# One encoder trunk: probabilities times V in plain FP32 for the mLSTM and dilated heads

## The chip, the cores and the metric

The kernel runs on one core of a Trainium2 chip. The metric is the device time of one execution in microseconds (us), taken as the median of several executions. The profiled execution is a run of its own and has its own time.

## The reference

Two layers of a hybrid encoder trunk act on two groups of tokens with the same weights, 256 of a prompt and 512 of a sample, 1024 channels each. Everything is FP32. Cut to what matters here, a layer is

```
z = rmsnorm(x) @ w_in                       # q, k, v of three head groups, gates
ya = dilated attention, 4 heads of 64       # mixture of three windows, softmax
yb = mLSTM, 4 heads of 64                   # gated weights, forward plus backward, no softmax
yc = grouped attention, 8 query heads on 2 k/v heads
x += concat(ya, yb, yc) @ w_out
x += cross attention into 256 memory tokens, 4 heads
x += (silu(conv3(gate)) * val) @ w_down     # gate, val = rmsnorm(x) @ w_up
```

In each head a matrix P of (queries x keys) is formed and multiplied with V (keys x 64). P is a softmax in the dilated, grouped and cross heads, and a gated, normalised score matrix in the mLSTM.

## The kernel before

Channels lie on the partitions and the 768 tokens along the columns: first the 256 of the prompt, then the 512 of the sample. `STREAMS` holds both as (start, length), the sample first. A projection is done in the type FP32R, in which one matmul carries only a part of the bits of an FP32 number. Each operand is therefore split into a high part (a cast on ScalarE, `hi_op`) and the rest (a subtraction on VectorE, `tt`), and three matmuls are summed: high times high, high times rest, rest times high (`mm_chunks`, L208).

`attend` (L367) does one head on one stream. It forms the scores block by block in the PSUM bank S (two buffers), lets `soft` turn them into P in SBUF (tiles of 512 columns from the FP32 arena), and for the mLSTM waits until all rows are there and scales them (`settle_p`). Then, for each key block, it transposes P on TensorE into the bank T (two buffers, L392), casts the 512 columns into `ph` on ScalarE (L395) and subtracts on VectorE into `pl` (L396). Two FP32R matmuls accumulate into the bank Y (one buffer): V times `ph` (L400) and V times `pl` (L401). The weights are 128 wide: `v_tokens` (L340) has put V's high part into 64 of the columns and its rest into the other 64, in the order that depends on the head's place e in its pair. So one half of Y's partitions holds the product with the high part and the other that with the rest, and the end of `attend` adds them: a copy on ScalarE (L405) and an addition on VectorE (L406). For 512 tokens there are four blocks T and four key blocks; for 256 tokens one block T holds both key blocks.

A layer runs its heads in this order: grouped (c0, c1), mLSTM (b0, b1), dilated (a0, a1), two heads to a pair for b and a. `ahead` (L353) writes a later pair's projections first in the program but gives the attention of the pair before a higher priority, so that projections fill the time between the steps of an attention. The order on each engine is fixed ahead of the run by a scheduler that simulates the kernel. Buffers come from arenas, lists of free column ranges in one large tile, of which the range freed longest ago is taken: `af` in FP32 (18 x 768 columns), `ar` in FP32R for the operands of matmuls, and `asm` of 4 x 512 columns for `ph` and `pl` alone. The feed-forward stage cuts its own arenas out of the same two large tiles (`ffn`, L1011), and one of them, `fw`, runs to the end of the FP32 tile.

V is projected by `v_proj` (L619): 10 and 11 are the column blocks of the mLSTM's V, 4 and 5 those of the dilated heads, 17 that of the grouped heads.

Of the kernel before, what the change touches and what calls it, by code (L numbers as in the profile page):

```python
# [9 lines left out]
F32 = mybir.dt.float32  # L10
# [25 lines left out]
N_IN = 21  # L36
N_HID = 21
HT = T // 2
HOT = 2000
CHUNKS = ((0, 1),) + tuple((c, c + 2) for c in range(1, 21, 2))  # L40

# [3 lines left out]
R_COLS = 18 * 768  # L45
S_COLS = 4 * 512
PREP = 7 * 512
F_COLS = 18 * 768
N_PAR = 143

K_ID, K_TRI, K_IND = 0, 128, 384
# [57 lines left out]
def trunk_kernel(ctx, tc, xT, memT, w_in, w_out, w_xq, w_xkv, w_xo, w_up, w_dn, w_dnt, par, fin_g, cst, fmk, tabs,  # L109
# [227 lines left out]
                      sub="%s%d%d" % (name, n, k % 4))  # L337
        return xh_s, xl_s

    def v_tokens(zv, nt, vv, site):  # L340
        for c0, n in (STREAMS if nt == 6 else ((0, 512),)):
            ps = small_ps(site, "vps")
            m = n // 128
            j0 = c0 // 128
            for i in range(m):
                PE.transpose(ps[:, i * 128:(i + 1) * 128], zv[:, c0 + i * 128:c0 + (i + 1) * 128], ident)
            for e in range(2):
                src = ps[:, :n].rearrange("p (i h d) -> p i h d", h=2, d=64)[:, :, e]
                a, b = 64 * e, 64 - 64 * e
                A.copy(vv[e][:, j0:j0 + m, a:a + 64], src)  # L350
                tt(vv[e][:, j0:j0 + m, b:b + 64], src, vv[e].bitcast(F32)[:, j0:j0 + m, a:a + 64], ALU.subtract)
# [15 lines left out]
    def attend(qs, q0, nq, KH, KL, k0, nk, vv, vt0, e, y, y0, soft, settle_p=None):  # L367
# [14 lines left out]
            held.append(pt)  # L382
        if settle_p:
            settle_p(ptiles)
        yps = bank("Y", "yps")
        nkt = nk // 128
        nb = 512 // n
        for kb in range(0, nkt, nb):
            t = bank("T", "t")
            for j in range(nb):  # L390
                for i in range(nq):
                    PE.transpose(t[:, j * n + i * 128:j * n + (i + 1) * 128],  # L392
                                 ptiles[i][:, (kb + j) * 128:(kb + j + 1) * 128], ident)
            ph, pl = asm.tile(512), asm.tile(512)
            hi_op(pick("ph_" + SITE[0], "A"), ph, t)  # L395
            tt(pl, t, ph.bitcast(F32), ALU.subtract)  # L396
            for j in range(nb):
                kt = kb + j
                w = vv[:, vt0 + kt]
                PE.matmul(yps[:, :n], w, ph[:, j * n:(j + 1) * n], start=kt == 0, stop=False)  # L400
                PE.matmul(yps[:, :n], w, pl[:, j * n:(j + 1) * n], start=False, stop=kt == nkt - 1)  # L401
            asm.free(ph, pl)
        af.free(*held)
        yo = y[64 * e:64 * e + 64, y0:y0 + n]
        hi_op(pick("yo_" + SITE[0], "A"), yo, yps[64 - 64 * e:128 - 64 * e, :n])  # L405
        tt(yo, yps[64 * e:64 * e + 64, :n], yo, ALU.add)  # L406

# [110 lines left out]
    def mixers(l, xt, x_dram, stats):  # L518
# [100 lines left out]
        def v_proj(t):  # L619
            zv = ft()  # L620
            proj(w_in[l, t], xh, xl, ev_to(zv, "v%d" % t), sub="w_v%d" % t)
            vv = [rtl(), rtl()]
            v_tokens(zv, 6, [tok(v) for v in vv], "v%d" % t)
            af.free(zv)
            return vv
# [43 lines left out]
        def c_attn(g, qr):  # L669
# [4 lines left out]
            for hh in range(4):  # L674
# [2 lines left out]
                           plain_soft(den[:, hh, c0 // 128:(c0 + n) // 128, g],  # L677
                                      lambda i, ni, hh=hh, c0=c0: rq8[:, c0 // 128 + i:c0 // 128 + i + ni, hh]))
                ar.free(qs[hh])
            ar.free(K, vv)  # L680

        def stacks(qq, kk):
            out = []
# [50 lines left out]
        def b_attn(pb, sv):  # L734
            SITE[0] = "b%d" % pb
            sts, vv, rows = sv
            for e in range(2):
                qs, K = sts[e]
                hd = 2 * pb + e
                for c0, n in STREAMS:  # L740
                    gb = rows[e][:, 2 * c0:2 * c0 + 2 * n].rearrange("p (d k) -> p d k", d=2)
                    attend(qs, c0, n // 128, K[:, :T], K[:, T:], c0, n, tok(vv[e]), c0 // 128, e, yt[5 + pb], c0,
                           *b_soft(gb, c0, n, hd))
                af.free(rows[e])
                ar.free(qs, K, vv[e])

        def b_soft(gb, c0, n, hd):
            nq, t0 = n // 128, c0 // 128
# [74 lines left out]
        def a_attn(pg, sv, order, last=True):  # L823
# [5 lines left out]
                       mask_soft(C["fm"], den[:, 4 + pg, c0 // 128:(c0 + n) // 128, e]))  # L829
            if last:  # L830
                for e in range(2):
                    ar.free(*sts[e], vv[e])

        ths = []

# [608 lines left out]
```

## Time and profile before

| | us |
|---|---|
| median of three executions | 2137.96 (2136.34 to 2138.89) |
| profiled execution, whole | 2145.01 |
| its span, first to last instruction | 2143.2 |
| TensorE (PE) busy | 2003.8 |
| VectorE (DVE) busy | 1841.7 |
| ScalarE (ACT) busy | 1061.7 |

PE busy counts a matmul from its start to its modelled end, and the next one starts before that. So 100% is reached while matmuls still follow each other at their own pace, and the distance between two starts is the better measure of what a matmul costs. The granted clock is the share of 2.4 GHz that TensorE was given, as a mean over a stretch: 1.00 is 2.4 GHz throughout, 0.50 is 1.2 GHz throughout.

### The profile page before, as it was taken

What the parts mean: (1) busy time and instruction counts of PE and PEld (TensorE: products, weight loads), DVE (VectorE), ACT (ScalarE), POOL (GpSimd) and SP (SyncE); (2) the same over time, 40 slices, a digit from 0 to 9 for tenths busy, and PEclk for the clock granted to TensorE, in tenths of its full rate; (3) what the DMA queues carried; (4) which work ended last, traced back from release to release, by engine and by line L of the source; (5) the groups of instructions that cost most, each with busy time, mean ns of one, the idle gap of its engine ahead of it and who ended that gap; (6) DMA issues with size and microseconds to landing.
All of it is one profiled execution on the core that took longest, in us unless ns stands there. A gap on an engine that the chain in (4) does not pass through costs nothing.

```text
span 2143.2 us, 31059 instructions
## 1 busy us (share of the span) xinstructions
PE 2003.8 (93%) x11280; PEld 1782.8 (83%) x11280; DVE 1841.7 (86%) x3822; ACT 1061.7 (50%) x2119; POOL 7.8 (0%) x32
## 2 busy tenths in 40 slices
PE   7989989998899999999999897999988999999997
PEld 5878768787789999999888775777877999999995
DVE  8787887867999999999977868778779999999998
ACT  4257767547533333333534667565665333333342
POOL 0000000000000000000000000000000000000000
PEclk8989989999999999999999998999999999999998
DMA  5433335342132212212254314343421222222202
GB/s 179 138 82 101 96 89 124 110 132 80 50 90 79 67 62 72 74 63 88 65 179 117 92 44 107 99 111 123 124 64 56 83 70 69 70 69 70 69 30 79
DMA packets 62953, 190.94 MB, mean 89 GB/s; under 512 B 8072, under 2 KB 11400, under 8 KB 62032
## 3 DMA queue, kind: packets, MB, share of 16 engines
q1 hardware_dynamic: 62800, 188.96, 30.1%
q8 instruction: 89, 1.46, 0.3%
q14 instruction: 64, 0.52, 0.1%
HBM read 145.97 MB, written 10.71 MB: 73 GB/s over the span
## 4 chain that ended last, share of the span: by engine, by line
PE 74%; DVE 16%; ACT 4%; DMA 3%; issue 2%; SPq 1%; POOL 0%; DVEq 0%; ACTq 0%
PE rps L1105 8%; PE rps L1107 8%; PE rps L1106 8%; PE rps L1148 5%; PE rps L1149 5%; PE rps L1150 5%; PE prS L213 4%; PE prS L214 4%; PE prS L215 4%; DVE arena_f L158 4%; PE t L392 3%; PE prP L213 2%; PE prP L214 2%; PE prP L215 2%; DVE arena_r L158 2%
## 5 line engine op out<-in xcount | busy, mean ns | idle before, releaser
L158 DVE TENSOR_TENSOR arena_f<-arena_f 128x512 f32<-128x512 f32 (+2 forms) x373 | 265.6, 728 | 27.7 <-DMA arena_f<-arena_f 15.2
L183 ACT CAST wh<-arena_f 128x512 fp32r<-128x512 f32 x266 | 162.2, 621 | 253.0 <-PE rps L1106 212.8
L183 ACT CAST wh<-wr 128x512 fp32r<-128x512 f32 x260 | 159.4, 620 | 236.3 <-PE rps L1106 98.9
L158 DVE TENSOR_TENSOR xall<-rps,xall 128x512 f32<-128x512 f32 (+1 forms) x384 | 197.9, 549 | 14.1 <-PE rps L1150 6.9
L1148 PE MATMUL rps<-arena_r,wh 128*128 128x512 f32 (+1 forms) x608 | 202.6, 339 | 3.4 <-DVE xall L158 3.2
L158 DVE TENSOR_TENSOR wl<-wr,wh 128x512 fp32r<-128x512 f32 x264 | 179.5, 683 | 29.5 <-ACT wh L183 27.9
L1105 PE MATMUL rps<-xha,wh 128*128 128x384 f32 x608 | 203.9, 335 | 0.5 <-ACT wh L183 0.4
L1106 PE MATMUL rps<-xla,wh 128*128 128x384 f32 x608 | 203.4, 335 | 0.0
L1149 PE MATMUL rps<-arena_r,wh 128*128 128x512 f32 (+1 forms) x608 | 201.2, 338 | 0.0
L1107 PE MATMUL rps<-xha,wl 128*128 128x384 f32 x608 | 199.2, 334 | 0.0
L213 PE MATMUL prS<-xha,wh 128*128 128x512 f32 x480 | 188.8, 397 | 3.1 <-DVE arena_f L158 1.0
L215 PE MATMUL prS<-xha,wl 128*128 128x512 f32 x480 | 189.1, 396 | 1.5 <-DVE wl L158 1.5
L214 PE MATMUL prS<-xla,wh 128*128 128x512 f32 x480 | 189.9, 396 | 0.0
L158 DVE TENSOR_TENSOR wl<-arena_f,wh 128x512 fp32r<-128x512 f32 x266 | 179.2, 684 | 1.5 <-ACT wh L183 1.3
L1150 PE MATMUL rps<-arena_r,wl 128*128 128x512 f32 (+1 forms) x608 | 178.3, 339 | 0.0
L158 DVE TENSOR_TENSOR arena_f<-rps,arena_f 128x384 f32<-128x384 f32 x266 | 143.6, 552 | 28.2 <-PE rps L1107 26.0
L1105 PE MATMUL rps<-arena_r,wh 128*128 128x384 f32 x456 | 152.8, 335 | 0.0
L1106 PE MATMUL rps<-arena_r,wh 128*128 128x384 f32 x456 | 152.3, 334 | 0.0
L158 DVE TENSOR_TENSOR arena_r<-t,arena_r 128x512 fp32r<-128x512 f32 x184 | 124.9, 683 | 27.8 <-ACT arena_r L183 24.4
L213 PE MATMUL prP<-xha,wh 128*128 128x256 f32 x480 | 138.9, 289 | 9.8 <-DVE xall L158 5.9
L1107 PE MATMUL rps<-arena_r,wl 128*128 128x384 f32 x456 | 146.4, 334 | 0.0
L392 PE MATMUL t<-cs,arena_f 128*128 128x128 f32 x736 | 125.6, 291 | 13.9 <-DVE arena_r L158 7.5
(235 smaller groups left out, 5004.7 us busy)
## 6 DMA issues: line engine op xcount, KB each, us to landing
arena_f<-in_w_up SPq DMA_DIRECT2D x76, 512.0 KB, 3.6
wr<-in_w_in SPq DMA_DIRECT2D x42, 512.0 KB, 3.6
wr<-in_w_dn SPq DMA_DIRECT2D x40, 512.0 KB, 3.7
wr<-in_w_out SPq DMA_DIRECT2D x32, 512.0 KB, 5.2
arena_r<-arena_r SPq DMA_DIRECT2D x32, 384.0 KB, 6.7
arena_r<-arena_r SPq DMA_DIRECT2D x48, 192.0 KB, 4.0
xall<-in_xT SPq DMA_DIRECT2D x8, 768.0 KB, 8.7
arena_r<-arena_r SPq DMA_DIRECT2D x64, 96.0 KB, 2.2
```

The lines of the kernel that those rows point to most:

```text
L158: V.tensor_tensor(out, a, b, op=op)
L183: A.copy(out, a)
L213: PE.matmul(ps, h[:, j], xh[i][:, c0:c0 + n], start=i == 0, stop=False)
L214: PE.matmul(ps, h[:, j], xl[i][:, c0:c0 + n], start=False, stop=False)
L215: PE.matmul(ps, lo[:, j], xh[i][:, c0:c0 + n], start=False, stop=i == tot - 1)
L392: PE.transpose(t[:, j * n + i * 128:j * n + (i + 1) * 128], ptiles[i][:, (kb + j) * 128:(kb + j + 1) * 128], ident)
L1105: PE.matmul(ps, h[:, k], x[k], start=k == 0, stop=False)
L1106: PE.matmul(ps, h[:, k], x[4 + k], start=False, stop=False)
L1107: PE.matmul(ps, lo[:, k], x[k], start=False, stop=k == 3)
L1148: PE.matmul(ps, h[:, m], hh[i][:, c], start=k == 0 and not tail, stop=False)
L1149: PE.matmul(ps, h[:, m], hlo[i][:, c], start=False, stop=False)
L1150: PE.matmul(ps, lo[:, m], hh[i][:, c], start=False, stop=i == b - 1)
```

## The change

For the sites b0, b1, a0 and a1 V is kept as plain FP32 in one tile for both heads of a pair, the transposed P is copied once to an FP32 tile, and one plain FP32 matmul with 64 columns of weights writes the 64 partitions of Y that the head needs; one copy takes them out. The grouped heads and the cross attention stay as they were. V and `ph` of these sites move from `ar` and `asm` to `af`, and `af` grows by 512 columns. Frees that only follow from this are left out of the diff below.

```diff
@@
+FULL = ("b0", "b1", "a0", "a1", )
+FULL_V = (10, 11, 4, 5, )
@@
-F_COLS = 18 * 768
+F_COLS = 18 * 768 + 512
@@ v_tokens
+            if full:
+                A.copy(vv[:, j0:j0 + m], ps[:, :n].rearrange("p (i d) -> p i d", d=128))
+                continue
             for e in range(2):
@@ attend
+        full = SITE[0] in FULL
         yps = bank("Y", "yps")
@@
-            ph, pl = asm.tile(512), asm.tile(512)
-            hi_op(pick("ph_" + SITE[0], "A"), ph, t)
-            tt(pl, t, ph.bitcast(F32), ALU.subtract)
+            if full:
+                ph = af.tile(512)
+            else:
+                ph, pl = asm.tile(512), asm.tile(512)
+            if full:
+                A.copy(ph, t)
+            else:
+                hi_op(pick("ph_" + SITE[0], "A"), ph, t)
+                tt(pl, t, ph.bitcast(F32), ALU.subtract)
             for j in range(nb):
                 kt = kb + j
+                if full:
+                    PE.matmul(yps[64 * e:64 * e + 64, :n], vv[:, vt0 + kt, 64 * e:64 * e + 64],
+                              ph[:, j * n:(j + 1) * n], start=kt == 0, stop=kt == nkt - 1)
+                    continue
                 w = vv[:, vt0 + kt]
                 PE.matmul(yps[:, :n], w, ph[:, j * n:(j + 1) * n], start=kt == 0, stop=False)
                 PE.matmul(yps[:, :n], w, pl[:, j * n:(j + 1) * n], start=False, stop=kt == nkt - 1)
@@
         yo = y[64 * e:64 * e + 64, y0:y0 + n]
+        if full:
+            A.copy(yo, yps[64 * e:64 * e + 64, :n])
+            return
         hi_op(pick("yo_" + SITE[0], "A"), yo, yps[64 - 64 * e:128 - 64 * e, :n])
         tt(yo, yps[64 * e:64 * e + 64, :n], yo, ALU.add)
@@ v_proj
+            if t in FULL_V:
+                vf = ft()
+                v_tokens(zv, 6, tok(vf), "v%d" % t, True)
+                af.free(zv)
+                return [vf, vf]
             vv = [rtl(), rtl()]
```

## Rows read from the trace of the kernel before

**Rows 1.** The page, part 1: span, and busy time of each engine.
```profile
span 2143.2 us, 31059 instructions
PE 2003.8 (93%) x11280; PEld 1782.8 (83%) x11280; DVE 1841.7 (86%) x3822; ACT 1061.7 (50%) x2119; POOL 7.8 (0%) x32
```
**Rows 2.** Busy time by stage; the columns: stretch, length, engines, clock, DMA share, GB/s.
```profile
80.00:245.00 165.00, 154.97 (x894) 131.95 (x893) 133.70 (x263) 101.20 (x215) 1.12 (x12) 0.96 0.38 99
245.00:335.00 90.00, 76.33 (x392) 61.05 (x391) 78.18 (x278) 67.20 (x169) 2.76 (x2) 0.87 0.35 90
335.00:425.00 90.00, 85.47 (x497) 71.27 (x496) 74.36 (x191) 55.94 (x126) 0.00 (x0) 0.98 0.45 121
640.00:1000.00 360.00, 360.00 (x2069) 343.49 (x2068) 342.89 (x581) 133.92 (x204) 0.00 (x0) 1.00 0.22 69
1130.00:1290.00 160.00, 148.42 (x841) 125.53 (x840) 123.66 (x245) 96.84 (x207) 0.99 (x12) 0.96 0.30 80
1290.00:1380.00 90.00, 73.01 (x368) 57.64 (x367) 71.91 (x268) 61.42 (x156) 1.38 (x1) 0.85 0.40 102
1380.00:1480.00 100.00, 92.42 (x527) 75.28 (x526) 79.36 (x203) 60.90 (x137) 1.39 (x1) 0.98 0.42 113
```
**Rows 3.** The same view, stretches of 10 us inside the mLSTM heads.
```profile
250.00:260.00 10.00, 7.98 (x34) 5.58 (x33) 9.54 (x34) 9.41 (x27) 0.00 (x0) 0.83 0.29 59
310.00:320.00 10.00, 6.63 (x29) 4.69 (x28) 9.90 (x45) 7.75 (x21) 0.00 (x0) 0.89 0.76 186
1310.00:1320.00 10.00, 5.14 (x14) 2.67 (x14) 6.46 (x35) 5.25 (x15) 0.00 (x0) 0.50 0.47 132
```
**Rows 4.** Who waited for whom, TensorE: total us, times, longest.
```profile
PE yps L400 <- DVE xall L158: 12.1, 9, 3.4
PE s L378 <- DVE dn L769: 9.5, 9, 3.0
```
**Rows 5.** Groups by shape: VectorE's work; busy us, mean ns, then idle before.
```profile
L158 DVE TENSOR_TENSOR arena_r<-t,arena_r 128x512 fp32r<-128x512 f32 x184 | 124.9, 683 | 27.8 <-ACT arena_r L183 24.4 <-PE yps L401 2.4
L158 DVE TENSOR_TENSOR xall<-yps,xall 64x512 f32<-64x512 f32 x32 | 22.0, 686 | 4.7 <-ACT xall L183 4.1
L158 DVE TENSOR_TENSOR xall<-yps,xall 64x256 f32<-64x256 f32 x32 | 13.3, 417 | 4.9 <-ACT xall L183 4.4
L158 DVE TENSOR_TENSOR arena_r<-vps,arena_r 128x256 fp32r<-128x256 f32 x28 | 11.7, 419 | 6.1 <-ACT arena_r L350 5.9
L158 DVE TENSOR_TENSOR arena_r<-vps,arena_r 128x128 fp32r<-128x128 f32 x20 | 5.6, 279 | 0.1
```
**Rows 6.** The same view: ScalarE's cast of T, FP32R and FP32 matmuls.
```profile
L183 ACT CAST arena_r<-t 128x512 fp32r<-128x512 f32 x184 | 105.5, 584 | 50.8 <-PE t L392 31.1 <-PE yps L400 17.4 <-DVE nt L161 1.2
L400 PE MATMUL yps<-arena_r 128*128 128x512 f32 x144 | 65.3, 453 | 7.6 <-ACT arena_r L183 5.4 <-DVE xall L158 2.1
L268 PE MATMUL cps<-cs,arena_f 128*128 128x1 f32 x92 | 11.8, 244 | 2.3 <-DVE arena_f L158 2.2
```
**Rows 7.** TensorE in order of time: start us, us, line, tile, shape.
```profile
303.09 0.40 PE L213 MATMUL prS<-xha,wh 128*128 128x512 f32 x1
303.32 0.40 PE L214 MATMUL prS<-xla,wh 128*128 128x512 f32 x1
...
311.56 0.60 PE L346 MATMUL vps<-cs,arena_f 128*128 128x128 f32 x4
311.92 0.48 PE L215 MATMUL prS<-xha,wl 128*128 128x512 f32 x1
312.23 0.40 PE L213 MATMUL prS<-xha,wh 128*128 128x512 f32 x1
312.47 0.40 PE L214 MATMUL prS<-xla,wh 128*128 128x512 f32 x1
```
**Rows 8.** Busy time by stage again: the feed-forward stage's first part, each layer.
```profile
560.00:600.00 40.00, 34.97 (x199) 30.52 (x199) 37.65 (x89) 17.74 (x33) 0.00 (x0) 0.91 0.20 61
1600.00:1640.00 40.00, 30.86 (x169) 25.98 (x168) 35.73 (x90) 21.65 (x47) 0.00 (x0) 0.87 0.12 40
```

More of the change, by code (lines that the diff above doesn't have):

```diff
@@ L338, in split_x, with v_tokens @@
         return xh_s, xl_s
-    def v_tokens(zv, nt, vv, site):
+    def v_tokens(zv, nt, vv, site, full=False):
         for c0, n in (STREAMS if nt == 6 else ((0, 512),)):
@@ L401, in attend @@
                 PE.matmul(yps[:, :n], w, pl[:, j * n:(j + 1) * n], start=False, stop=kt == nkt - 1)
-            asm.free(ph, pl)
+            if full:
+                af.free(ph)
+            else:
+                asm.free(ph, pl)
         af.free(*held)
         yo = y[64 * e:64 * e + 64, y0:y0 + n]
+        if full:
+            A.copy(yo, yps[64 * e:64 * e + 64, :n])
+            return
         hi_op(pick("yo_" + SITE[0], "A"), yo, yps[64 - 64 * e:128 - 64 * e, :n])
@@ L679, in c_attn @@
                 ar.free(qs[hh])
-            ar.free(K, vv)
+            ar.free(K)
+            if "c0" not in FULL:
+                ar.free(vv)
+            elif g:
+                af.free(vv)
         def stacks(qq, kk):
@@ L744, in b_attn @@
                 af.free(rows[e])
-                ar.free(qs, K, vv[e])
+                ar.free(qs, K)
+                if "b%d" % pb not in FULL:
+                    ar.free(vv[e])
+                elif e:
+                    af.free(vv[e])
         def b_soft(gb, c0, n, hd):
@@ L831, in a_attn @@
                 for e in range(2):
-                    ar.free(*sts[e], vv[e])
+                    ar.free(*sts[e])
+                    if "a%d" % pg not in FULL:
+                        ar.free(vv[e])
+                    elif e:
+                        af.free(vv[e])
         ths = []
```

## The prediction

> **What bounds the kernel now.** I read the page's first part, then busy time by stage, then the shapes that the edit touches. On the whole span TensorE is busy 2003.8 of 2143.2 us and VectorE 1841.7 [rows 1], so both count, and a mean over the span can't say which one a stage waits for. By stage [rows 2] the reader should see three kinds. The feed-forward stage is TensorE throughout: 360 of 360 us, clock 1.00. The stages with the dilated heads (335 to 425 us, 1380 to 1480 us) are nearly so: 85.5 of 90 and 92.4 of 100, clock 0.98. The stages with the mLSTM heads (245 to 335 and 1290 to 1380 us) are not: TensorE 76.3 and 73.0 of 90, clock 0.87 and 0.85, while VectorE has 78.2 and 71.9. Inside these the 10 us stretches alternate: in some VectorE is full (9.54 and 9.90 of 10) and TensorE idles, in one neither is (6.46 and 5.14) and the granted clock is 0.50, its level of 1.2 GHz, after TensorE had idled [rows 3]. TensorE's waits there end with VectorE: the score matmuls wait 9.5 us in all for the mLSTM's gating (it holds bank S), and the products with V wait 12.1 us, all heads together, for the addition that empties the single bank Y [rows 4].
>
> I use one figure for each stage: TensorE's busy time times its clock, over the length, its density. mLSTM: 76.33 x 0.87 = 66.4 of 90 = 0.738, and 73.01 x 0.85 = 62.1 of 90 = 0.690. Dilated: 83.8 of 90 = 0.931, and 90.6 of 100 = 0.906. The grouped heads before them: 148.8 of 165 = 0.902, and 142.5 of 160 = 0.890 [rows 2].
>
> **The change part by part.** *Off VectorE.* Sixteen heads are touched (four mLSTM and four dilated, two layers), each with four blocks T for the sample and one for the prompt: 80 blocks. The subtraction into `pl` goes: 80 x 0.683 = 54.6 us. The additions at the end go: 16 x (0.686 + 0.417) = 17.6 us. V: eight tiles, each two subtractions of 0.419 (sample) and two of 0.279 (prompt): 8 x 1.396 = 11.2 us [rows 5]. Sum 83.4 us, some 21 us in each of the four stages (of 72 to 79 that VectorE works there).
>
> *ScalarE.* The cast of T (0.584 us, [rows 6]) becomes a copy of the same size, the copy out of Y stays, and V's four half copies become two whole ones. I put this at nothing; ScalarE has 56 to 67 us of work in these stages of 90 to 100 [rows 2], which is the cover. Bank T is released after 0.584 instead of 0.584 + 0.683 us, and Y after the copy alone.
>
> *On TensorE.* Two FP32R matmuls of N columns become one plain FP32 matmul. FP32R of 512 columns starts every 0.23 us (303.09 to 303.32, [rows 7]), so a block costs 2 x 0.23 = 0.46 us now. The trace has no wide plain FP32 matmul; the nearest are the column sums with one to four columns. The 46 calls with one column (four for the memory, six for each of seven norms) leave 92 records, while the 144 FP32R products with V leave 144 [rows 6]: a plain FP32 matmul runs as two. What one of the two costs over 512 columns is the open price. Lower bound: one stream of columns each, 0.46 us a block, nothing added. Upper bound: this kernel shows that an FP32 number takes two FP32R parts, hence a full product four products of parts. Before, two of them lie side by side in 128 weight columns, so two streams do. With 64 weight columns nothing lies side by side, and four streams are 4 x 0.23 = 0.92 us, +0.46 a block, 80 x 0.46 = 36.8 us, 9.2 us in each stage. I take the upper bound, because the one number the records show, two, fits the weights being split and leaves the moving side to be split too. The Trainium skill, page "FP8 and Floating Point Precision", section "TensorE Precision Notes", lists "True FP32: 4 passes through PE array". By it the sum would be the same 36.8 us; no row here shows it.
>
> *Switches.* After four FP32 transposes the next FP32R matmul starts on time, but the one behind it starts 0.31 us later instead of 0.23 (311.92 to 312.23, then 312.47, [rows 7]): 0.08 us for a change of kind. The new product is a kind with 64 output columns that the trace doesn't have. Bounds: 80 fewer changes between transposes and products, -6 us; or two changes around each of 80 blocks, +13 us. I take 0, since the order on TensorE already alternates kinds; both ends go to the range. The Trainium skill, page "TensorEngine Tiling (Array Packing)", section "Key Properties", says that changing the tiling mode drains TensorE, which speaks against 64-column weights among 128-column ones; no row shows a drain for it, and by it one would be nearer to the upper end.
>
> *Buffers.* During b0's attention `af` holds two pairs of gate rows (2 x 3072 columns). Now two V tiles of 768 are added, and each head takes five `ph` of 512: free for P, the gate products and `ph` are 14336 - 6144 - 1536 = 6656 columns against 7680, while a head's demand goes from 4096 (2048 + 1024 for the sample, 512 + 512 for the prompt) to 6656. So a range comes round after one head instead of nearly two. That binds a head's first exponentials to the transposes of the head before, which are over by then unless the filler's tiles lie between. I take 0; upper end in the second rival. `asm` and `ar` get emptier, which costs nothing.
>
> *Feed-forward stage.* `fw` gains 512 columns, and the arena for its first terms holds a third tile of 1536 (4864 columns against 4352). Its first part leaves TensorE idle 5.0 and 9.1 us of 40 [rows 8]; later there is no idle time to win [rows 2]. Bounds -5 to +3 us, I take 0, because the waits there aren't shown to be for a buffer.
>
> **The sum.** TensorE's work at full clock becomes 75.6, 93.0, 71.3 and 99.8 us (each +9.2). What length this gives depends on the density. In the dilated stages VectorE's relief (74.4 to 53, 79.4 to 58) lets me put 0.95, little above 0.931: 97.9 (+7.9) and 105.1 (+5.1). In the mLSTM stages the gating, the exponentials and the scaling remain, about half of the stretches are bound by them, and only the rest gains; I put the middle between the present density and 0.93, 0.834 and 0.81: 90.6 (+0.6) and 88.0 (-2.0). Sum +11.6 us. The profiled execution took 2145.0 (span 2143.2 and 1.8 around it), 7.0 above the median of 2138.0; the difference is put on both: 2156.6 for a like profiled run, 2149.6 for the median.
>
> **Rivals.** *One: the relief wins, the time falls.* In the mLSTM stages VectorE sets the pace; with 21 us less of it the added matmuls fall into idle time and hold the clock up. With 0.95 in all four stages: 79.6 + 97.9 + 75.0 + 105.1 = 357.6 against 370, -12.4 us: 2125.6. For it: VectorE at 9.54 and 9.90 of 10, and the waits of 9.5 and 12.1 us [rows 3, 4]. Against: in the stretch at clock 0.50 neither engine is full, so the chain of one head's steps, not VectorE's amount of work, is late. It decides from the point where the mLSTM stages reach about 0.90.
>
> *Two: nothing is filled.* The waits stay because they belong to the gating, and the arena ties heads closer. At today's densities: 102.4 + 99.9 + 103.3 + 110.2 = 415.8, +45.8 us: 2184. For it: the gating isn't touched. Against: 21 us less on an engine at 80% should not go for nothing.
>
> *Three: the change doesn't cost what it says,* two streams instead of four. Work as today at the forecast's densities: 79.6 + 88.2 + 76.7 + 95.4 = 339.9, -30 us: 2108. For it: two records. Against: the four products of parts.
>
> **How the numbers follow.** Forecast 0.53, first rival 0.22, second 0.17, third 0.08. The forecast's own range, with the switches (-6 to +13) and the feed-forward stage (-5 to +3), is 2138 to 2166. The range that holds 8 in 10 takes in most of the first rival and half of the second: 2120 to 2180. About 0.2% (4.3 us) is what a measurement can tell from no change. Faster than 2133.7: the first rival nearly whole, and the third, 0.27. Within: the forecast's low end and the rest of the first, 0.17. Slower: 0.56.
>
> **What would show it.** Each FP32 product of 512 columns should take 0.92 us from start to start, in two records of 0.46; 0.46 in all would prove the third rival. VectorE should be busy 83 us less in the whole span, ScalarE the same. The dilated stages should be longer by 5 to 8 us each, the mLSTM stages about as long, with density 0.81 to 0.84. The wait for VectorE ahead of products with V should be gone for these heads; late next should be TensorE itself in the dilated stages, and the gating in the mLSTM ones. It would be wrong if the scheduler's new order moves time in the grouped heads or the feed-forward stage, which I hold unchanged.

## The result, and the profile of the changed kernel

The median went from 2138.43 us (2136.34 to 2144.28) to 2163.17 us (2160.57 to 2165.29): +24.7 us, a ratio of 1.0111 with a 95% interval of 1.0088 to 1.0134. It is slower, as forecast, but by more than twice the forecast's +11.6. The two profiled executions show less of it than the medians: before's (2145.0) lies 6.6 above its median, the changed one's (2160.6) 2.6 below, so what follows from the two traces explains 15.6 us, and sizes of single effects are taken from runs further down.

The page of the changed kernel, part 1, answers to [rows 1]:

```profile
span 2158.8 us, 30798 instructions
PE 2034.6 (94%) x11280; PEld 1758.5 (81%) x11280; DVE 1778.8 (82%) x3678; ACT 1060.3 (49%) x2103; POOL 7.9 (0%) x32
```

VectorE has lost the 144 instructions that the prediction counted (80 + 32 + 32), ScalarE stands still, TensorE is busy 30.8 us more. Groups by shape (busy us, mean ns, then idle before), which answer to [rows 5] and [rows 6]:

```profile
L412 PE MATMUL yps<-arena_f 128*64 128x512 f32 x128 | 68.8, 623 | 2.4 <-ACT arena_f L405 1.7 <-issue 0.6
L412 PE MATMUL yps<-arena_f 128*64 128x256 f32 x64 | 17.2, 392 | 0.4 <-ACT arena_f L405 0.4
L160 DVE TENSOR_TENSOR arena_r<-t,arena_r 128x512 fp32r<-128x512 f32 x104 | 70.2, 684 | 17.4 <-ACT arena_r L185 17.1
L405 ACT COPY arena_f<-t 128x512 f32<-128x512 f32 x80 | 45.2, 583 | 41.7 <-PE t L398 40.8 <-DVE arena_r L163 0.8
```

The new product stands there: 192 records, two for each of 64 products with 512 columns and 32 with 256. The subtraction has gone from 184 to 104, and the ScalarE copy takes what the cast took, 583 against 584 ns. The busy time of a group overlaps from matmul to matmul, so the price is read from starts. TensorE in order of time (start us, us, line, tile, shape), which answers to [rows 7]:

```profile
344.44 0.28 PE L216 MATMUL prP<-xla,wh 128*128 128x256 f32 x1
344.65 1.07 PE L412 MATMUL yps<-arena_f 128*64 128x512 f32 x2
345.65 0.33 PE L398 MATMUL t<-cs,arena_f 128*128 128x128 f32 x1
345.91 1.07 PE L412 MATMUL yps<-arena_f 128*64 128x512 f32 x2
346.92 0.98 PE L398 MATMUL t<-cs,arena_f 128*128 128x128 f32 x7
```

From a product's start to the next instruction's start: 1.00 us (344.65 to 345.65, 345.91 to 346.92). The FP32R pair that it replaces takes 0.46. (The matmul ahead, with 256 columns, takes 0.21 until the product starts; what that means comes with the price.)

Now the stages. I cut both traces at the same events, since fixed times no longer mean the same work: from the transposes of the mLSTM's gates to the last scores of the cross attention (the mLSTM and dilated heads lie in it, and fillers for them), and from there to the first matmul of the feed-forward part that repeats; I call these the attention stage and the lead-in (of the feed-forward stage). Columns as in [rows 2]. Before:

```profile
153.00:526.00 373.00, 345.75 (x1992) 293.18 (x1990) 293.03 (x753) 246.49 (x572) 3.55 (x10) 0.95 0.38 104
526.00:604.00 78.00, 67.71 (x378) 57.29 (x378) 73.18 (x159) 44.57 (x93) 0.00 (x0) 0.96 0.24 72
1197.00:1584.00 387.00, 350.26 (x1990) 294.39 (x1990) 292.83 (x753) 245.63 (x572) 3.29 (x8) 0.95 0.37 101
1584.00:1663.00 79.00, 66.69 (x375) 56.35 (x373) 71.78 (x157) 42.79 (x89) 0.00 (x0) 0.94 0.20 66
```

And the changed kernel:

```profile
151.00:539.00 388.00, 363.37 (x1990) 282.12 (x1988) 260.35 (x681) 245.52 (x561) 3.36 (x8) 0.98 0.38 101
539.00:619.00 80.00, 69.98 (x378) 58.93 (x379) 71.08 (x157) 44.56 (x93) 0.00 (x0) 0.94 0.19 56
1209.00:1590.00 381.00, 362.29 (x1988) 279.79 (x1986) 260.03 (x679) 244.55 (x561) 3.55 (x10) 0.98 0.38 102
1590.00:1679.00 89.00, 73.25 (x387) 62.10 (x386) 74.95 (x163) 46.78 (x96) 0.00 (x0) 0.88 0.19 60
```

The reader should first see that the cuts fit: 1990 and 1988 TensorE instructions in the attention stage against 1992 and 1990. In it TensorE works 17.6 and 12.0 us more, its clock rises from 0.95 to 0.98, and VectorE works 33 us less in each layer. The same edit has opposite results in the two layers: by the exact events 372.6 became 388.2 (+15.6) and 387.7 became 381.5 (-6.2), +9.4 together. The lead-ins, where nothing was edited, grew from 157.0 to 167.8 together (+10.8), the second at a clock of 0.88. The two stretches with the grouped heads lost 4.8, the repeating feed-forward part changed by 0.0, and the end lost 2.9; with what lies after TensorE's last instruction that is the 15.6 us of the spans.

TensorE's waits (total us, times, longest), which answer to [rows 4]:

```profile
PE bps L318 <- ACT arena_f L313: 14.6, 5, 4.2
PE yps L417 <- DVE arena_r L160: 9.4, 11, 1.6
PE yps L416 <- DVE xall L160: 8.5, 5, 3.4
PE s L383 <- DVE dn L804: 6.0, 8, 1.5
PE yps L412 <- ACT arena_f L405: 2.0, 2, 1.7
```

The wait for the addition that empties Y is left only at L416, the heads that still use two parts (12.1 became 8.5), and the gating costs 6.0 instead of 9.5. The new products wait 2.0 us in all. At the top now are the norms' scale (L318) and the low parts of the heads that weren't edited (L417).

To see what the price and the relief are I summed TensorE's time over the whole traces, each instruction from its start to the next start, less the time in which the engine idled: plain FP32 products with V 0 before, 80.9 us after; FP32R work, put at 0.23 us for 512 columns, 1755.4 and 1718.6 (-36.8, the 80 pairs of 0.46); the transposes of P into T 82.3 and 82.4; other plain FP32 matmuls (V's transposes, norms, gates) 58.1 and 55.5; what FP32R matmuls took beyond that pace (low clock, changes of kind) 108.1 and 97.2; idle 137.9 and 122.7. So the price in the products is 80.9 - 36.8 = +44.1, and the other lines give back 28.6.

### The profile page after: what moved, and what is told of

Same layout as the page of the kernel before. It is cut to its first block, busy times and chain, and to the rows that moved or that the text cites. A ratio compares the mean times of both kernels' runs of the same rounds, so it can differ in the third digit from the quotient of the medians.

```text
span 2158.8 us, 30798 instructions
## 1 busy us (share of the span) xinstructions
PE 2034.6 (94%) x11280; PEld 1758.5 (81%) x11280; DVE 1778.8 (82%) x3678; ACT 1060.3 (49%) x2103; POOL 7.9 (0%) x32
## 4 chain that ended last, share of the span: by engine, by line
PE 79%; DVE 12%; ACT 4%; DMA 2%; issue 2%; SPq 0%; POOL 0%; DVEq 0%; ACTq 0%; POOLq 0%
PE rps L1146 8%; PE rps L1144 8%; PE rps L1145 8%; PE prS L215 5%; PE prS L217 5%; PE prS L216 5%; PE rps L1187 5%; PE rps L1188 5%; PE rps L1189 5%; PE yps L412 3%; DVE arena_f L160 3%; PE t L398 3%; PE prP L215 3%; PE prP L216 2%; PE prP L217 2%
## 5 line engine op out<-in xcount | busy, mean ns | idle before, releaser
L160 DVE TENSOR_TENSOR arena_f<-arena_f 128x512 f32<-128x512 f32 (+3 forms) x373 | 267.0, 733 | 12.8 <-DMA arena_f<-arena_f 5.9
L398 PEld LDWEIGHTS t<-cs,arena_f 128*128 128x128 f32 x736 | 89.7, 144 | 68.8 <-issue 40.9
L217 PE MATMUL prP<-xha,wl 128*128 128x256 f32 x480 | 138.5, 289 | 0.2 <-DVE wl L160 0.2
```

What stands on the lines that cost most here:

```text
L160: V.tensor_tensor(out, a, b, op=op)
L217: PE.matmul(ps, lo[:, j], xh[i][:, c0:c0 + n], start=False, stop=i == tot - 1)
L398: PE.transpose(t[:, j * n + i * 128:j * n + (i + 1) * 128], ptiles[i][:, (kb + j) * 128:(kb + j + 1) * 128], ident)
```

## The experiments

My theory after the result had three parts: a price of plain FP32 (four streams, plus something for the form with 64 weight columns), a relief from VectorE's missing work, and a rest from elsewhere. The rivals: that the products are dear for another reason, that VectorE's relief brings nothing, or that arena and buffers make the loss. Ratios are against the kernel before in the same session; differences in us between experiments are differences of ratios times 2141.

**Buffers first.** The arena alone, on the kernel before:

```diff
-F_COLS = 18 * 768
+F_COLS = 18 * 768 + 512
```

> The kernel before with the FP32 arena 512 columns larger and nothing else. In the two traces the grouped, mLSTM and dilated stages together are 1.6 us shorter after the change, while the stage with the output projection and the cross attention and the first part of the feed-forward stage are 17 us longer, although nothing in them was edited. Theory A (price): the added time is the plain FP32 product, 1.00 us a block in the trace after against 0.46, partly hidden; the larger arena does nothing: 2134 to 2143 us. Theory B (arena): the larger arena changes which ranges are reused and so the waits in the unedited stages: 2148 to 2158 us.

Measured 2148.11 us against 2140.97, ratio 1.0035 (1.0015 to 1.0055). With no arithmetic changed, +7.5 us (ratio times 2141). The other way round, the changed kernel with the feed-forward arenas cut out of the old width:

```diff
+        FC = F_COLS - 512
-        fw = Arena(f_all[:, 2 * PREP:], F_COLS - 2 * PREP)
+        fw = Arena(f_all[:, 2 * PREP:], FC - 2 * PREP)
...
```

> The changed kernel, with the feed-forward stage cutting its arenas out of the first 18 x 768 columns as before; only the stages ahead of it see the 512 more. Theory A (price): as the changed kernel, 2159 to 2167 us. Theory B (arena): the first part of the feed-forward stage loses its 10 us again, 2148 to 2156 us; the cross attention, which still sees the larger arena, keeps its own.

Measured 2165.45, ratio 1.0114 (1.0097 to 1.0131): the same as the whole change (1.0111). The longer lead-in isn't made by the feed-forward arenas.

**The relief without the price** (the relief run, from here on). V and `ph` in FP32R, and two FP32R matmuls on the same operands:

```diff
-                ph = af.tile(512)
+                ph = asm.tile(512)
...
-                    PE.matmul(yps[64 * e:64 * e + 64, :n], vv[:, vt0 + kt, 64 * e:64 * e + 64],
-                              ph[:, j * n:(j + 1) * n], start=kt == 0, stop=kt == nkt - 1)
+                    w, p = vv[:, vt0 + kt], ph[:, j * n:(j + 1) * n]
+                    PE.matmul(yps[:, :n], w, p, start=kt == 0, stop=False)
+                    PE.matmul(yps[:, :n], w, p, start=False, stop=kt == nkt - 1)
```

> The changed kernel with the price of the product put back: for the mLSTM and dilated heads V and the transposed P are cast to FP32R once, and two FP32R matmuls with the same operands and 128 weight columns stand for the plain FP32 one. The products with the low parts are left out, and the product of the high parts is counted twice. ScalarE and VectorE do what they do after the change; TensorE does what it did before. Theory A (price): 80 blocks at 0.46 instead of 1.00 us, 43 us less TensorE work than the changed kernel, of which what the relief can't hide comes back: 2110 to 2130 us, that is below the kernel before. Theory B (arena or a new order in the unedited stages): still 10 to 17 us above what the relief alone would give, 2135 to 2150 us.

Measured 2106.86 against 2140.97, ratio 0.9843 (0.9829 to 0.9858): -34 us. Its page:

```profile
span 2105.4 us, 30770 instructions
PE 1981.6 (94%) x11280; PEld 1776.2 (84%) x11280; DVE 1773.7 (84%) x3678; ACT 1056.6 (50%) x2103; POOL 8.4 (0%) x32
```

and its attention stage in both layers:

```profile
153.00:509.00 356.00, 333.61 (x1992) 287.79 (x1991) 258.27 (x682) 244.20 (x562) 3.25 (x7) 0.98 0.40 109
1183.00:1544.00 361.00, 337.67 (x1985) 290.30 (x1985) 257.11 (x679) 242.80 (x561) 3.35 (x8) 0.97 0.39 106
```

The stage is 17 and 26 us shorter than before (by the exact events 716.9 in all, -43.4), VectorE's work is that of the changed kernel, and TensorE's falls with the higher clock. So the relief is real and large, which speaks against the second rival of the prediction. The lead-ins are longer here too, 164.9 against 157.0, with no plain FP32 product with V in the kernel: of the +10.8 that they grew after the change, 7.9 are already in this run's -34.

Putting the 80 subtractions back into the changed kernel, with a result that nobody reads:

```diff
+                pl = asm.tile(512)
+                tt(pl, t, ph, ALU.subtract)
+                asm.free(pl)
```

> The changed kernel with the 80 subtractions on VectorE put back, into a range that nobody reads; the sum is as after the change. 54.6 us of VectorE work return. If the relief was worth something where VectorE sets the pace (theory A): 10 to 30 us above the changed kernel, 2173 to 2193 us. If the relief fell into time in which VectorE was not waited for (rival): within 4 us of the changed kernel, 2159 to 2167 us.

Measured 2175.14, ratio 1.0159 (1.0144 to 1.0174), 10 us over the changed kernel: 54.6 us of VectorE's work are worth about a fifth of their length. And the opposite edit on the kernel before, the same subtractions dropped and with them the product with the low part of P:

```diff
+            lone = SITE[0][0] in "ab"
-            tt(pl, t, ph.bitcast(F32), ALU.subtract)
+            if not lone:
+                tt(pl, t, ph.bitcast(F32), ALU.subtract)
...
+                if lone:
+                    continue
```

> The kernel before without the low part of the transposed P in the mLSTM and dilated heads (that part of the sum is left out): one FP32R matmul a block, V's high and low part in its 128 weight columns as before, the addition at the end and V's split as before. VectorE loses the 80 subtractions of 54.6 us, TensorE 80 x 0.23 = 18 us. It says what the relief is worth when TensorE gets less work too: 34 us x 54.6/83.4 = 22 of relief and up to 18 of TensorE, 2100 to 2118 us.

Measured 2119.12 against 2142.64, ratio 0.9886 (0.9870 to 0.9901), -24 us, with one FP32R stream a block left. That is 1 us above the expected range. TensorE has 18.4 us less to do; if these count in full, 6 us are left for the 54.6 us of VectorE. Both runs put the subtractions at 6 to 10 us, where their share of VectorE's 83.4 us would be 22 of the relief run's 34. Which of its other parts (the additions, V's halves, the shorter way from T and Y to what follows, another order) bring the rest isn't shown.

Moving the subtraction to GpSimd instead of dropping it (kernel before; ScalarE copies T to SBUF first):

```diff
+                tf = af.tile(512)
+                A.copy(tf, t)
+                G.tensor_tensor(pl, tf, ph.bitcast(F32), op=ALU.subtract)
+                af.free(tf)
```

> The kernel before with the 80 subtractions of the mLSTM and dilated heads moved from VectorE to GpSimd, which can't read PSUM: ScalarE copies T a second time, to SBUF, and GpSimd subtracts there. TensorE's work is that of before. VectorE loses 54.6 us; ScalarE gains 80 copies of 0.58 us (46 us, on an engine that is 56 to 67 percent busy in these stages). If the relief carries over: two thirds of the 34 us that it was worth, 2112 to 2130 us. If ScalarE and the longer way to the low part become the wait: 2135 to 2160 us.

Measured 2168.91, ratio 1.0125 (1.0098 to 1.0153). It is slower, outside both expected ranges. The GpSimd subtractions and the page's engines:

```profile
L399 POOL TENSOR_TENSOR arena_r<-arena_f,arena_r 128x512 fp32r<-128x512 f32 x80 | 106.6, 1341 | 317.4 <-ACT arena_f L398 201.4 <-DVE dn L775 47.0 <-PE yps L406 21.9
PE 2015.9 (93%) x11280; PEld 1792.5 (83%) x11280; DVE 1832.6 (84%) x3742; ACT 1100.6 (51%) x2199; POOL 114.5 (5%) x112
```

A subtraction takes 1341 ns here, against 683 on VectorE. But VectorE doesn't get the relief: its busy time falls by 9.1 us (1841.7 to 1832.6), not by 54.6. The 80 subtractions are gone, but the instructions whose count stayed take 37.6 us longer. The subtraction into `wl`, both of whose operands lie in SBUF, takes 1094 ns in the 12 cases that run mostly beside a GpSimd subtraction, and 686 in the other 252; an operation of 512 columns that reads the scores from PSUM takes 688 (16 cases) and 685 (24). ScalarE has 80 copies more. TensorE waits directly for GpSimd's result only 4.5 us in all:

```profile
PE yps L407 <- POOL arena_r L399: 4.5, 7, 1.4
```

So this run moves the load and doesn't take it off. It can't say whether a block's longer way from T to its product, VectorE's slower instructions or ScalarE's copies make the loss.

**The price.** 128 weight columns instead of 64, otherwise the changed kernel:

```diff
-                    PE.matmul(yps[64 * e:64 * e + 64, :n], vv[:, vt0 + kt, 64 * e:64 * e + 64],
-                              ph[:, j * n:(j + 1) * n], start=kt == 0, stop=kt == nkt - 1)
+                    PE.matmul(yps[:, :n], vv[:, vt0 + kt], ph[:, j * n:(j + 1) * n],
+                              start=kt == 0, stop=kt == nkt - 1)
```

> The changed kernel with all 128 columns of the FP32 V (both heads of the pair) as weights, so that the plain FP32 product fills all 128 partitions of Y, and only the needed half is copied out. The sum is the same; TensorE streams as many columns but never meets a 64-column form. Theory A (four streams, whatever the width): a block still takes about 1.00 us from start to start and the time stays at 2158 to 2170 us. Theory C (the 64-column form costs a drain at each change): 80 blocks lose 0.08 to 0.16 us each, 2150 to 2158 us, and a block shows 0.92 us or less.

Measured 2152.52 against 2141.25, ratio 1.0052 (1.0034 to 1.0070): 12.6 us less than the change, with twice the weight columns. Two products in a row in its timeline:

```profile
348.58 0.47 PE L216 MATMUL prS<-xla,wh 128*128 128x512 f32 x1
348.89 1.88 PE L412 MATMUL yps<-arena_f 128*128 128x512 f32 x4
350.61 0.60 PE L398 MATMUL t<-cs,arena_f 128*128 128x128 f32 x4
```

348.89 to 350.61 is 1.72 us for two, 0.86 each instead of 1.00. And half of the columns with 64 weight columns:

```diff
+                    h = n // 2
-                    PE.matmul(yps[64 * e:64 * e + 64, :n], vv[:, vt0 + kt, 64 * e:64 * e + 64],
-                              ph[:, j * n:(j + 1) * n], start=kt == 0, stop=kt == nkt - 1)
+                    PE.matmul(yps[64 * e:64 * e + 64, :h], vv[:, vt0 + kt, 64 * e:64 * e + 64],
+                              ph[:, j * n:j * n + h], start=kt == 0, stop=kt == nkt - 1)
...
```

> The changed kernel with the plain FP32 product over the first half of the query columns only (its result is copied to both halves, so half of the products are left out). Everything else, types, buffers, copies, 64 weight columns, is as after the change. Theory A (streamed columns are the price): a block falls from 1.00 to about 0.55 us, TensorE has what it had before the change, and the time falls to near the run with two FP32R streams (2107): 2105 to 2122 us. Rival (a fixed cost for each FP32 product or the fuller FP32 arena is a good part of the price): 2125 to 2150 us, with a block above 0.65 us for the fixed cost, or at 0.55 us for the arena.

Measured 2138.44, ratio 0.9985 (0.9974 to 0.9997). In its timeline:

```profile
340.71 0.65 PE L413 MATMUL yps<-arena_f 128*64 128x256 f32 x2
341.29 0.55 PE L398 MATMUL t<-cs,arena_f 128*128 128x128 f32 x3
341.76 0.65 PE L413 MATMUL yps<-arena_f 128*64 128x256 f32 x2
342.34 0.77 PE L398 MATMUL t<-cs,arena_f 128*128 128x128 f32 x5
```

0.58 us for 256 columns (340.71 to 341.29, 341.76 to 342.34). Two lengths and two widths give the price: 256 columns more cost 1.00 - 0.58 = 0.42 us, so 512 columns stream in 0.84, and 1.00 - 0.84 = 0.16 is fixed. The 128-wide product has nearly no fixed part: 0.86 in all. The granted clock is 1.00 in these stretches, so 0.86 us are 2064 cycles of 2.4 GHz, four for each of the 512 columns, where FP32R's 0.23 us are about one: four streams. The Trainium skill, page "FP8 and Floating Point Precision", section "TensorE Precision Notes", gives four passes for true FP32, and these traces agree. The fixed part of 0.14 to 0.16 us belongs to the form with 64 weight columns between matmuls of 128. The Trainium skill, page "TensorEngine Tiling (Array Packing)", section "Key Properties", says that changing the tiling mode drains TensorE; the trace agrees with a cost of that kind, and it shows one on the way in as well as on the way out. The same sequence in the changed kernel and then in the 128-wide one, both at clock 1.00:

```profile
351.32 0.39 PE L215 MATMUL prS<-xha,wh 128*128 128x512 f32 x1
351.55 0.39 PE L216 MATMUL prS<-xla,wh 128*128 128x512 f32 x1
351.87 1.07 PE L412 MATMUL yps<-arena_f 128*64 128x512 f32 x2
352.87 0.66 PE L398 MATMUL t<-cs,arena_f 128*128 128x128 f32 x4
```

```profile
320.44 0.39 PE L383 MATMUL s<-arena_r 128*128 128x512 f32 x1
320.67 0.39 PE L384 MATMUL s<-arena_r 128*128 128x512 f32 x1
320.90 1.02 PE L412 MATMUL yps<-arena_f 128*128 128x512 f32 x2
321.76 0.60 PE L398 MATMUL t<-cs,arena_f 128*128 128x128 f32 x4
```

The FP32R matmul just ahead of the product takes 0.32 us instead of 0.23, the product 1.00 instead of 0.86, the four transposes behind it 0.66 instead of 0.60. Where the clock was full, the matmul ahead took 0.093 us over its pace on average in the changed kernel (40 cases) and 0.004 in the 128-wide one (34); the first transpose behind took 0.056 over the others' time (35 cases) and nothing (36). So a lone product with 64 weight columns costs about 0.3 us for its form, and its own 1.00 us shows half of that.

Where TensorE's time went, in us of each trace, summed as above:

| | before | changed | relief run | 128 wide |
|---|---|---|---|---|
| plain FP32 products with V | 0 | 80.9 | 0 | 68.8 |
| FP32R at 0.23 us for 512 columns | 1755.4 | 1718.6 | 1755.4 | 1718.6 |
| FP32R beyond that pace | 108.1 | 97.2 | 94.4 | 96.8 |
| transposes into T | 82.3 | 82.4 | 78.0 | 79.1 |
| other plain FP32 | 58.1 | 55.5 | 54.0 | 54.0 |
| idle | 137.9 | 122.7 | 122.3 | 132.0 |

From the relief run to the changed kernel the span grows by 53.4 us: 44.1 are the products, 8.7 other work on TensorE, and 0.4 idle time. In these two traces the loss isn't waiting; TensorE does more. The changed kernel goes into the products 77 times, and 77 x (0.09 + 0.06) = 12 us, an estimate from the cases above, is of the size of the 8.7. By the same rows the 52.8 us of work part in two: 35.5 from the relief run to the 128-wide kernel, the four streams, and 17.3 from there to the changed kernel, the form with 64 columns (12.1 of them stand on the products' row). The 17.3 aren't given back whole: the 128-wide kernel has 9.3 us more idle time than the changed one, and its span is 8.1 shorter.

**One site at a time.** Only the dilated heads, then only the mLSTM heads (there with `ar` 512 wider and `af` 448, to make room):

```diff
-FULL = ("b0", "b1", "a0", "a1", )
-FULL_V = (10, 11, 4, 5, )
+FULL = ("a0", "a1", )
+FULL_V = (4, 5, )
```

> The change for the dilated heads alone. Price: half of the 58 us that separate the changed kernel from the one with two FP32R streams, 29 us. Relief: these stages were TensorE's (95 and 92 percent busy), so I expect less than half of the 34 us, about 10: 2141 + 19 = 2160, range 2152 to 2166 us. If the relief is spread evenly (17 us): 2153 us or less.

Measured 2150.66 against 2141.25, ratio 1.0039 (1.0025 to 1.0052): +8.4, where the forecast has +13.0 for these stages; it is what a relief spread evenly would give.

```diff
-FULL = ("b0", "b1", "a0", "a1", )
-FULL_V = (10, 11, 4, 5, )
+FULL = ("b0", "b1", )
+FULL_V = (10, 11, )
-R_COLS = 18 * 768
+R_COLS = 18 * 768 + 512
-F_COLS = 18 * 768 + 512
+F_COLS = 18 * 768 + 448
```

> The change for the mLSTM heads alone (the FP32R arena had to grow by 512 columns and the FP32 arena by 448 for all tiles to find a range). The change on the dilated heads alone gave 9.4 us. If the parts add up, 23.5 - 9.4 = 14 us: 2152 to 2158 us, and the mLSTM heads, where the relief should have counted most, cost more than the dilated ones. By the prediction (mLSTM stages about even): 2139 to 2146 us.

Measured 2167.55 against 2142.90, ratio 1.0111 (1.0088 to 1.0135): +24, where the forecast has -1.4. The parts sum to +32, the whole is +24. They don't add up, and the second has other arenas, so this doesn't say what the mLSTM heads cost; it was a first sign that orders or arenas move as much as the edit does.

**Room or order?** The relief run once more, with the columns held in `af` that the change holds there (768 for each V, 512 for each block) and not used:

```diff
-                ph = asm.tile(512)
+                ph, idle = asm.tile(512), af.tile(512)
...
                 vf = rtl()
+                spare[t] = ft()
```

> The run with two FP32R streams (2107 us) left V and the transposed P in the FP32R arenas. This one holds ranges of the same size in the FP32 arena for as long as the change does (768 columns for each V, 512 for each block), without using them, so that P and the gate products get the ranges that they get after the change. TensorE, VectorE and ScalarE do exactly what they do in that run (the same products are left out). The run with half of the columns came out 31 us above it with only 8 us more between starts of the products, so some 20 us have another cause. Theory D (the fuller FP32 arena: ranges come round sooner and P waits for older work): 2120 to 2132 us. Theory E (the arena is harmless; what the plain FP32 product itself does to the order on the engines is the cause): 2103 to 2112 us.

Measured 2115.23 against 2142.90, ratio 0.9861 (0.9839 to 0.9883): 4 us over the run without, between the two expected ranges, and the intervals overlap. Then more room for the changed kernel, 960 columns instead of 512:

```diff
-F_COLS = 18 * 768 + 512
+F_COLS = 18 * 768 + 960
```

> The changed kernel with 448 more columns in the FP32 arena (960 more than before, all that SBUF has left). Theory D: 448 of the roughly 2048 columns that the change takes come back, so about a fifth of 20 us, 2157 to 2163 us, if it is proportional; Theory E: 2160 to 2169 us, as the changed kernel. This run alone can't separate them if the gain is small; it is the other side of the run with held ranges.

Measured 2156.69 against 2142.90, ratio 1.0054 (1.0038 to 1.0069): 12 us less than the change, and just under both expected ranges. The 128-wide and then the half-width kernel, each with this line changed as well:

> The changed kernel with 128 weight columns and the FP32 arena at 960 more columns than before. Apart, the wide form took 12 us off the changed kernel (1.0114 to 1.0052 of the kernel before) and the larger arena 12 us (to 1.0054). If they are two causes, price of the 64-column form and room in the arena, they add: about 1.000 of the kernel before, 2137 to 2147 us. If each was only a luckier order, no sum is due: 2148 to 2160 us.

Measured 2140.65 against 2142.64, ratio 0.9988 (0.9978 to 0.9997), again 14 us less than with 512. It is the fastest version found that does all of the work, level with the kernel before.

> The run with half of the query columns (half of the products are left out; 2138 us) with the FP32 arena at 960 more columns. Between it and the run with two streams and held ranges (2115) lie 23 us, of which about 10 are TensorE's own (48.6 us in the products against 38 in that run). Arena theory: the ranges of V and of the transposed P are really used here and come round sooner than idle ones, so more room gives back 8 to 15 us: 2123 to 2131 us. If the rest belongs to the plain FP32 product (its changes of kind on TensorE): within 4 us of 2138.

Measured 2129.87 against 2142.64, ratio 0.9940 (0.9924 to 0.9957), 10 us less. Three times 10 to 14 us for the same 448 columns looked like want of room. Two controls speak against that reading. The kernel before with 960 columns more:

```diff
-F_COLS = 18 * 768
+F_COLS = 18 * 768 + 960
```

> The kernel before with the FP32 arena 960 columns larger and nothing else, the control for the runs with the larger arena. With 512 more columns it was 7 us above the kernel before. If room itself is worth something only where the change has filled the arena: within 8 us of the kernel before, 2138 to 2150 us. If 960 columns simply lead to a better order in any kernel, then 8 us or more below: under 2134 us, and the gain of 12 us is no sign of a full arena.

Measured 2181.02 against 2141.49, ratio 1.0178 (1.0152 to 1.0203): +38 us, with no arithmetic changed and more room. Its attention stage in both layers:

```profile
151.00:542.00 391.00, 351.04 (x2005) 297.68 (x2006) 296.91 (x760) 251.04 (x581) 3.25 (x7) 0.94 0.36 99
1215.00:1612.00 397.00, 350.61 (x1985) 296.11 (x1985) 293.04 (x750) 246.42 (x571) 3.35 (x8) 0.93 0.36 98
```

18 and 10 us longer than before, and its waits:

```profile
PE yps L401 <- DVE arena_r L158: 16.3, 13, 4.3
PE s L378 <- DVE dn L769: 14.4, 11, 5.0
PE yps L400 <- ACT arena_r L183: 10.8, 6, 3.5
PE yps L400 <- DVE xall L158: 3.0, 4, 1.7
```

The first and third before, where [rows 4] has the other two:

```profile
PE yps L401 <- DVE arena_r L158: 3.5, 8, 0.7
PE yps L400 <- ACT arena_r L183: 5.4, 4, 2.5
```

The same instructions as before (VectorE 3822, TensorE 11280) wait 16.3, 14.4 and 10.8 us where they waited 3.5, 9.5 and 5.4, and 3.0 where they waited 12.1; TensorE's idle time is 28.3 us longer in all. The result lies outside both expected ranges. The order of TensorE's instructions is another one: it leaves that of the kernel before at the 152nd instruction, and 8325 of 11280 stand in the same place (7988 in the control with 512 columns). And the relief run with held columns, its `F_COLS` changed from + 512 to + 960:

> The run with two FP32R streams and held ranges (2115 us; the same products left out) with 960 instead of 512 more columns. If the 8 us between it and the run without held ranges (2107) are want of room, half or more come back: 2105 to 2111 us. If they are only another order: 2111 to 2119 us.

Measured 2116.99 against 2141.49, ratio 0.9883 (0.9853 to 0.9913): no gain against 512 columns. So the width of an arena acts here as another set of ranges, from which the scheduler makes another order of the whole run. In the kernel before, that was worth +7.5 and +38 us; whether the gains of 10 to 14 come from the order or from the room isn't shown. The 128-wide kernel was also run once more: a single execution of 2158.4 us where 2150 to 2157 was expected, with TensorE's instructions in the same order in all 11280 places. One execution adds nothing to the median of 2152.5, but it shows that one and the same order can come out 6 us apart in another session (the kernel before differs by 1.7 between the two).

## Why the prediction was right and where it was wrong

*VectorE, -83.4 us: right.* The five groups that shrank lose 54.7 + 17.6 + 11.1 = 83.4 us. The busy time of the page falls by 62.9 only: the instructions whose count stayed took 13.6 us longer in this execution (0.4 in the relief run), and the records overlap less.

*The step that failed: "Switches ... I take 0", and with it the price on TensorE.* Four streams of the moving operand, against two that the records might have meant, are confirmed. The forecast put them at 0.92 us and the new form at nothing, "since the order on TensorE already alternates kinds": +36.8 in all. The runs show +52.8: 44.1 in the products and 8.7 around them. The streams alone, with 128 weight columns, are +35.5, nearly the forecast's 36.8 (0.86 us a product instead of 0.92, and 3.5 us more in the work around them). What was missed is the form with 64 weight columns, +17.3 us, on the product itself and on the instructions ahead and behind. That is above the upper bound of +13, which took the 0.08 us of a change between kinds that all have 128 weight columns: a lone product pays about 0.3 us, not 0.16. The sentence on the drain had pointed the right way.

*The relief: as large as I gave, or larger.* The forecast holds 36.8 - 11.6 = 25.2 us of relief; the relief run shows 34, the two runs with held columns 30 and 25. The chain of a head's steps had been the argument for a small relief in the mLSTM stages. It got shorter as well, since T and Y are emptied by one instruction instead of two; how much of the relief is the chain's isn't shown.

*Density, the forecast's tool: fair.* In the attention stages busy time times clock over length went from 0.881 and 0.860 to 0.918 and 0.932. The forecast's edits, put on these longer stretches, give (328.5 + 18.4) / (373 + 8.5) = 0.909 and (332.7 + 18.4) / (387 + 3.1) = 0.900; the first rival's lengths give 0.936 and 0.931. The truth lay between in one layer and with the rival in the other. I had +8.5 and +3.1 for the two layers; +15.6 and -6.2 came.

*The sum.* The relief and the products alone give -34 + 44 = +10, next to the forecast's +11.6, but that is luck: the price is 7 above the forecast's and the relief 9. With the 8.7 around the products it is +19, and +24.7 was measured, so some 6 us are left. The same sum for the 128-wide kernel, 2106.9 + 35.5 = 2142.4, is 10 below its 2152.5; for that kernel with 960 columns, whose trace has 31.7 us more work on TensorE than the relief run's, 2138.6, it is 2 below its 2140.65.

*"Buffers, I take 0" and "Feed-forward stage, I take 0": too simple, but not the main part.* The prediction named a new order in stages held unchanged as what would make it wrong, but gave it no price. The reason for the zero, that the ranges come round late enough, was about room. What was missed is that a kernel whose order is made by a scheduler gets another order everywhere when buffers change. The kernel before has the shortest lead-ins: its two take 157.0 us together, less than in the trace of any of the 17 runs (160.6 to 170.7). No row of one trace could price that; the arena control does, +7.5 for these 512 columns with nothing else changed. It can't be added to the sum as it stands, since the relief run has the same 512 columns and its -34 holds what they did there.

*What stays open.* Where the last 6 us come from isn't shown. Counted from the runs with held columns instead, price and relief are -29.8 + 52.8 = +23 with 512 columns, where +24.7 was measured, and -25.0 + 52.8 = +28 with 960, where +12 was measured. The rest is +2 in one and -16 in the other, so it has no fixed sign, and whether room (for it: three kernels that gain 10 to 14 from 448 columns more) or the order alone (for it: the two controls) makes it isn't known. Running one order with the other arena would tell it and wasn't tried. Nor is it shown what the mLSTM heads cost alone.

*The rivals.* The first has its mechanism, the idle time is filled and the clock rises, but not its total: 2125.6 held the price at 36.8 and the rest at zero. The second (nothing filled, +45.8) falls with the relief run. The third (two streams) falls with 0.86 us a product; that the relief run measured 2106.9, near its 2108, fits, since that run is its mechanism built.

## What to carry to other kernels

Price a change of type on TensorE by the distance between starts, and bound its form as well: here plain FP32 took 0.86 us for 512 columns against 0.46 for the FP32R pair, and narrowing the weights to 64 columns added 0.14 instead of saving anything. Look at the instructions ahead and behind too: around a lone product they paid about as much again. Moving load to another engine isn't taking it away: with the subtractions on GpSimd, VectorE's busy time fell by 9 us instead of 55. And where a scheduler makes a new order for every change, run a control that changes only the buffers: here it moved the time by up to 38 us, more than the edit under test.

## What the runs showed of the hardware

Three things that I hadn't expected. A plain FP32 matmul shows as two records, but streams four times: four records of 512 columns take 1.72 us, 0.43 each, where an FP32R matmul takes 0.23. 64 weight columns instead of 128 cost 0.14 to 0.16 us more a product, at 256 columns (0.58 us) as at 512 (1.00), and some 0.09 us on the instruction ahead and 0.06 on a transpose behind. And while GpSimd subtracted, VectorE's subtractions of 512 columns with both operands in SBUF took 1094 ns instead of 686. A subtraction of 128x512 FP32 took 1341 ns on GpSimd (both operands in SBUF) and 683 on VectorE (one in PSUM).
